# Preparation of a half split in two, with its last eight products behind the buffers' wait, and stores to DRAM on GpSimd's queue

## The chip, the cores and the metric

The kernel runs on one core of a Trainium2 chip. Its engines have an instruction queue each and meet through semaphores: TensorE (PE; PEld is its weight load), VectorE (DVE), ScalarE (ACT), GpSimd (POOL), and SyncE (SP), which in this kernel does nothing but issue DMAs. The metric is device time in microseconds (us), the median of several runs.

## The reference

One layer of a hybrid decoder on T = 1056 tokens (a prompt of 1024, and 8 samples of 4), width 1024, all in float32:

```python
h = rmsnorm(x, norm_mix_g);  z = h @ w_in              # 1024 -> conv, r, k, v, LoRA inputs, gates
ya = silu(layernorm(causal_dwconv(glu(zc)))) @ w_conv_out
xs = zr + (prev - zr) * rw_mu                          # token shift, gives r, k, v, wl, al, gl
kk = normalize(k * rw_k_k);  k = k * (1 + (alr - 1) * rw_k_a)
S_t = S_{t-1} diag(w_t) + (S_{t-1} a_t) b_t^T + v_t k_t^T;  y_t = S_t r_t    # a = -kk, b = kk * alr
yb = ((groupnorm(y) + bonus) * gout) @ w_rw_out
x = x + (gate_a * ya + gate_b * yb) @ w_mix_out
x = x + ConvFFN(rmsnorm(x))                            # 1024 -> 2 x 3072 -> 1024
```

The recurrence on S, with 16 heads of size 64, is done in chunks of 64 tokens.

## The kernel before

Activations lie with channels on partitions and tokens along the free axis, in three blocks of 352 tokens. Each large product is made of three fp32r products (`mm3`: high x high, low x high, high x low), so one output tile of 128 channels is 3 x 3 x 8 = 72 matmuls of 352 columns.

`mixer_a` makes the convolution's inputs, the LoRA parts and the first r, k, v tiles, and stores them to DRAM (`d_cv`, `d_cum`, `d_alr`, `d_gout`, `d_rkv`). `mixer_b` computes the recurrence in 16 halves n (a half is 4 heads x 256 tokens; four halves in a row carry on the state of the same heads). A half goes through these steps:

- `prep(n)` loads k, cum, alr, r, v of the half from DRAM, and makes the decay P by exp (L911, after a memset of P's edges by GpSimd, L910), `kn`, the norms `nin` (L946 and on), the adjusted key `km`, the bonus `bv` (stored to `d_bv`, L977), and the operands E (E0, E1) and BK by products of 64 x 512 (L929, L988 to L990).
- `stage(n)` multiplies E by BK (`w<-E,BK`), takes the result off PSUM to LQ and E (L1012 to L1018; GpSimd clears the edges of LQ, L1015), stores LQ to `dL` (L1026), reads it back spread over 128 lanes as L (L1028), solves a triangular system there by 31 steps of `tm` = L x X (L1034) and X += tm (L1036) on DVE, and stores X to `dX` (L1038).
- `combine(n)` finishes the inverse with small products (D and LQ).
- `chain(n)` runs four chunks one after the other: c and R, UV, S, y. It ends with the eviction `Yev` (L1159).
- `group_norm(n)` normalizes Yev, adds `bvl`, multiplies by `gol`, and stores to `d_y` (L1203).

Around these run further streams: the samples (`samples_in`, `samples_steps`, `samples_state`), the convolution's layer norm (`ln_block`, from `d_cv` to `d_cs`, L399 and L416), the split of y (`s_y`) and the shift state. `drive` walks through the streams with a clock that counts the PE work issued so far. When no stream is due, it issues the next of the fillers: 18 r, k, v tiles (stored at L464), 16 gate tiles (L455), 8 tiles of the convolution's output. The waits between streams are names in a set; `s_prep` holds prep(n) back until chain(n-3) is done, since E and BK have three sets of buffers. L, X and tm have one buffer each. The list that results goes through a scheduler that sets the final order on each engine from dependences and buffers, so the order on one engine is not that of the source.

All DMAs but eight are issued by SP, in order: loads of weights and of the halves, the two passes dL and dX through DRAM that belong to the solve, and all stores. After the last chain come the merge, the mix, the FFN and the output: large products one after the other.

Of the kernel before, what the change touches and what calls it, by code (L numbers as in the profile page):

```python
# [31 lines left out]
class Net:  # L32
# [68 lines left out]
    def build(self):  # L101
        with ExitStack() as es:
# [6 lines left out]
            with ExitStack() as e1:  # L109
# [6 lines left out]
                with ExitStack() as e:  # L116
                    self.t4 = self.pool(e, "t4", 8)
                    self.mixer_a(w0)
# [231 lines left out]
    def conv_taps(self, cv, i):  # L350
# [18 lines left out]
        nc.sync.dma_start(out=self.d_cv[:, i], in_=c[:, :T])  # L369
# [17 lines left out]
    def ln_block(self, b):  # L387
# [28 lines left out]
        nc.sync.dma_start(out=self.d_cs[:, :, s], in_=C)  # L416
# [15 lines left out]
    def conv_out(self, i):  # L432
# [10 lines left out]
        nc.sync.dma_start(out=self.d_ma[i], in_=ga)  # L443
# [12 lines left out]

    def rkv_tile(self, j, n):
# [3 lines left out]
        t = self.T4("krv"[n])  # L461
        c0 = ZR + jj * 128
        yield from self.shifted(self.wjob(self.a["w_in"][0][:, c0:c0 + 128]), jj, t)
        nc.sync.dma_start(out=self.d_rkv[n][j // 2][:, j % 2], in_=t)  # L464
# [16 lines left out]
    def shifted(self, w, j, out, m=128):  # L481
# [6 lines left out]
        def ev(b, s, ps):  # L488
            t0 = b * BW
            nc.scalar.activation(out=out[:m, s], in_=ps, func=AF.Copy, scale=om)  # L490
            n = min(TP - t0, BW)
            add(out[:m, t0 + 1:t0 + n], ps[:, 0:n - 1])
            if b:
                add(out[:m, t0:t0 + 1], bc[:, b - 1:b])
            if n == BW:
                nc.vector.tensor_copy(out=bc[:, b:b + 1], in_=ps[:, n - 1:n])  # L496
            else:
                x = out[:m, TP:T].rearrange("p (b t) -> p b t", t=4)
# [4 lines left out]
                nc.vector.tensor_copy(out=self.shcol[:m, j, 1:9], in_=z[:, :, 3])  # L503
        yield from self.project_g(w, (self.hH, self.hL), 8, ev, m)
# [78 lines left out]
    def lora_out(self, j):  # L583
# [29 lines left out]
        for t, dst in ((cum, self.d_cum), (al, self.d_alr), (go, self.d_gout)):  # L613
            nc.sync.dma_start(out=dst[j // 2][:, j % 2], in_=t)
# [61 lines left out]
    T2N = 12  # L676

    def mixer_b(self):
# [6 lines left out]
        with ExitStack() as e:  # L685
            self.t4 = self.pool(e, "t4b", 2)
# [89 lines left out]
    def s_prep(self):  # L776
        for n in range(self.NH):
            k = [("rkv", j, x) for j in (n // 4 * 2, n // 4 * 2 + 1) for x in range(3)]
            if n > 2:
                k.append(("chain", n - 3))  # L780
# [4 lines left out]
            yield from self.prep(n)  # L785
            self.done.add(("prep", n))
# [47 lines left out]
    def s_shift(self):  # L834
# [3 lines left out]
        for g in range(7):  # L838
# [9 lines left out]
            nc.sync.dma_start(out=self.o["p_shift"][0][:, g * 512:g * 512 + n], in_=st[0:1, :n])  # L848
            nc.sync.dma_start(out=self.o["s_shift"][0][:, g * 512:g * 512 + n], in_=st[1:9, :n])
# [42 lines left out]
    def prep(self, n):  # L892
# [19 lines left out]
        PC = self.sm.tile([128, 8], F32, tag="PC", name="PC", bufs=3)  # L912
# [13 lines left out]
        E = [self.sg.tile([128, 8, 128], F32, tag=f"E{x}", name=f"E{x}") for x in range(2)]  # L926
# [11 lines left out]
        t2 = kn  # L938
        nc.vector.tensor_tensor(out=t2, in0=kn, in1=alr, op=ALU.mult)
# [5 lines left out]
        nin = self.sm.tile([128, 72], F32, tag="nin", name="nin", bufs=3)  # L945
# [21 lines left out]
        for u in range(2):  # L967
# [718 lines left out]
```

## Time and profile before

| | |
|---|---|
| median of 3 runs | 2556.56 us (2546.82 to 2561.31) |
| profiled execution | 2551.31 us, span 2549.6 us |
| mean granted clock of TensorE | 0.911 of full speed |
| busy: PE, DVE, ACT, POOL | 2372.1, 1645.4, 866.1, 91.9 us |
| first solve begins, last chain ends | about 352 us, 1379 us |

The sum of a stage is read from a view that gives each engine's busy time in a stretch; waits are put down to the instruction whose semaphore came last. Between 352 and 1379 us the 16 halves are worked off; before and after that the large products run with no recurrence beside them.

### The profile page before, as it was taken

Reading aid. Unit: us, or ns where it says so; the run is one execution under the profiler, and the core shown is the slowest. Engines: PE = TensorE matmul, PEld = TensorE weight load, DVE = VectorE, ACT = ScalarE, POOL = GpSimd, SP = SyncE. Lnnn points to the kernel's source line nnn. Section 1 sums busy time; section 2 is a strip of 40 time slices with the busy share of each in tenths; the row PEclk is TensorE's granted clock in tenths of the full one; section 3 lists DMA queues with packets and bytes.
Section 4 is the critical chain, followed back from the end, with each engine's and each line's share of the span. In section 5 each row is a group of like instructions: output and inputs, shape, how many; then the busy total and the mean of one; then the engine's idle time right before and its main releaser. Section 6 shows DMA issues by size and latency. Waiting matters only on the chain.

```text
span 2549.6 us, 41402 instructions
## 1 busy us (share of the span) xinstructions
PE 2372.1 (93%) x16094; PEld 2147.3 (84%) x16094; DVE 1645.4 (65%) x4174; ACT 866.1 (34%) x1716; POOL 91.9 (4%) x248
## 2 busy tenths in 40 slices
PE   6789989977798789898999999999999999999998
PEld 5778977766676577677778999999999999999998
DVE  5999766777767876786674344465554555545556
ACT  4234332433344344333344222333221322213225
POOL 2301100000000000000000000000000000000000
PEclk9999987966676788689999999999999999999999
DMA  4124443323232343434344664431111111111111
GB/s 123 48 82 161 157 115 83 89 69 100 77 98 63 81 115 85 104 92 117 85 114 137 215 188 137 127 128 44 44 47 48 43 51 44 47 47 40 54 51 69
DMA packets 307637, 230.61 MB, mean 90 GB/s; under 512 B 90492, under 2 KB 287123, under 8 KB 306921
## 3 DMA queue, kind: packets, MB, share of 16 engines
q1 hardware_dynamic: 307185, 227.80, 30.7%
q8 instruction: 127, 2.08, 0.3%
q14 instruction: 69, 0.57, 0.1%
q0 software_dynamic: 256, 0.17, 0.0%
HBM read 157.45 MB, written 70.45 MB: 89 GB/s over the span
## 4 chain that ended last, share of the span: by engine, by line
PE 58%; DVE 4%; DMA 3%; ACT 1%; issue 0%; SPq 0%; DVEq 0%; ACTq 0%
PE mm L54 50%; PE w L54 3%; DMA L<-dL 2%; PE c L54 1%; PE y L54 1%; PE w L61 1%; DMA hL<-d_y 1%; DVE tm L1034 0%; DVE X L1036 0%; PE w L1427 0%; PE w L1512 0%; DMA dX<-X 0%; DVE E L1018 0%; PE mm L1648 0%; PE w L1533 0%
## 5 line engine op out<-in xcount | busy, mean ns | idle before, releaser
L54 PE MATMUL mm<-hH,whi 128*128 128x352 f32 (+1 forms) x2568 | 878.1, 342 | 10.4 <-DVE bcol L496 9.1
L54 PE MATMUL mm<-hH,wlo 128*128 128x352 f32 (+1 forms) x2568 | 855.7, 335 | 20.6 <-DVE wlo L49 20.6
L54 PE MATMUL mm<-hL,whi 128*128 128x352 f32 (+1 forms) x2568 | 857.0, 334 | 0.2 <-DVE hL L248 0.2
L54 PEld LDWEIGHTS mm<-hH,whi 128*128 128x128 f32 (+1 forms) x2568 | 494.5, 193 | 38.3 <-DVE bcol L496 11.2
L54 PEld LDWEIGHTS mm<-hH,wlo 128*128 128x128 f32 (+1 forms) x2568 | 494.9, 193 | 33.0 <-DVE wlo L49 23.1
L54 PEld LDWEIGHTS mm<-hL,whi 128*128 128x128 f32 (+1 forms) x2568 | 495.9, 193 | 10.0 <-issue 1.2
L48 ACT ACTIVATE whi<-wraw 128x1024 fp32r<-128x1024 f32 (+2 forms) x123 | 126.0, 1025 | 403.5 <-PE mm L54 342.9
L1518 DVE TENSOR_TENSOR u<-mm,rs 128x352 f32<-128x352 f32 x144 | 73.5, 511 | 224.6 <-PE mm L54 224.5
L49 DVE TENSOR_TENSOR wlo<-wraw,whi 128x1024 fp32r<-128x1024 f32 (+2 forms) x123 | 146.2, 1189 | 67.8 <-ACT whi L48 67.7
L359 DVE SCALAR_TENSOR_TENSOR sg<-cu,par,sg 128x1024 f32<-128x1024 f32 x120 | 162.6, 1361 | 1.5
L54 PE MATMUL mm<-fH,whi 128*128 128x352 f32 x504 | 163.4, 324 | 0.0
L54 PE MATMUL mm<-fH,wlo 128*128 128x352 f32 x504 | 162.8, 323 | 0.0
L54 PE MATMUL mm<-fL,whi 128*128 128x352 f32 x504 | 162.7, 323 | 0.0
L1573 DVE TENSOR_TENSOR acc<-mm,acc 128x352 f32<-128x352 f32 x168 | 86.9, 522 | 94.0 <-PE mm L54 94.0
L1034 DVE TENSOR_TENSOR tm<-L,X 128x60 f32<-128x60 f32 (+24 forms) x496 | 101.4, 204 | 44.5 <-DMA L<-dL 39.4
L1548 DVE SCALAR_TENSOR_TENSOR c<-u,par,c 128x1024 f32<-128x1024 f32 x96 | 123.0, 1281 | 8.1 <-ACT c L1544 5.2
L54 PE MATMUL w<-E,BK 64*128 64x128 f32 x512 | 95.9, 348 | 17.8 <-DVE BK L990 11.7
L1109 ACT ACTIVATE SP<-UV,PC 64x64 f32<-64x64 f32 x192 | 64.8, 343 | 119.0 <-DVE UV L1149 104.8
L1036 DVE TENSOR_TENSOR X<-X,tm 128x60 f32<-128x60 f32 (+24 forms) x496 | 101.3, 204 | 5.1
L54 PEld LDWEIGHTS w<-E,BK 64*128 64x128 f32 x512 | 78.9, 239 | 29.9 <-DVE BK L990 12.3
L54 PE MATMUL y<-UV,E 128*64 128x64 f32 x512 | 75.8, 270 | 21.6 <-DVE UV L1149 18.4
L54 PEld LDWEIGHTS mm<-fH,whi 128*128 128x128 f32 x504 | 94.8, 188 | 0.5
(379 smaller groups left out, 3547.7 us busy)
## 6 DMA issues: line engine op xcount, KB each, us to landing
wraw<-w_in SPq DMA_DIRECT2D x50, 512.0 KB
wraw<-w_up SPq DMA_DIRECT2D x48, 512.0 KB
wraw<-w_down SPq DMA_DIRECT2D x32, 384.0 KB
L<-dL SPq DMA_DIRECT2D x16, 512.0 KB
d_alr<-la SPq DMA_DIRECT2D x8, 528.0 KB
d_cum<-lc SPq DMA_DIRECT2D x8, 528.0 KB
d_gout<-lg SPq DMA_DIRECT2D x8, 528.0 KB
d_k<-k SPq DMA_DIRECT2D x8, 528.0 KB
```

The lines of the kernel that those rows point to most:

```text
L48: nc.scalar.activation(out=hi[:, :nk, :m], in_=raw[:, :nk, :m], func=AF.Copy)
L49: (lo_eng or nc.vector).tensor_tensor(out=lo[:, :nk, :m], in0=raw[:, :nk, :m], in1=hi[:, :nk, :m].bitcast(F32), op=ALU.subtract)
L54: self.nc.tensor.matmul(out, l, r, start=start, stop=stop)
L61: self.nc.tensor.transpose(out, x, ident)
L359: nc.vector.scalar_tensor_tensor(out=c[:, 0:TP], in0=u[:, t:t + TP], scalar=self.col("conv_w", t * 4 + i), in1=c[:, 0:TP], op0=ALU.mult, o ...
L1034: nc.vector.tensor_tensor(out=tm[:, :a, :m], in0=L[:, s:s + 1, s + 1:32].to_broadcast([128, a, m]), in1=X[:, :a, s:s + 1].to_broadcast([12 ...
L1036: nc.vector.tensor_tensor(out=X[:, :a, s + 1:32], in0=X[:, :a, s + 1:32], in1=tm[:, :a, :m], op=ALU.add)
L1109: nc.scalar.activation(out=at(SP, u, x), in_=src(x)[:, u], func=AF.Copy, scale=PC[hs[x], 4 * u + c:4 * u + c + 1])
L1518: nc.vector.tensor_tensor(out=u[:, 2 + t0:2 + t0 + m], in0=p, in1=rs[:, t0:t0 + m], op=ALU.mult)
L1548: nc.vector.scalar_tensor_tensor(out=c[:, 0:TP], in0=u[:, t:t + TP], scalar=wt, in1=c[:, 0:TP], op0=ALU.mult, op1=ALU.add)
L1573: nc.vector.tensor_tensor(out=acc[i][:, s], in0=ps[:, :BW], in1=acc[i][:, s], op=ALU.add)
```

## The change

- `prep(n)` is split. What needs no buffer of the stage pool (loads, P, kn, nin, km, bv) no longer waits for chain(n-3). The eight products that write E and BK move into a new function `operands(n)`, issued after that wait. PC and nin get four buffers instead of three, and the T2 buffers are given back at other points.
- `t2` (kn x alr) and `km` are computed in place of alr and k: alr x k once, then a scaled copy and a multiply-add for km and a scaled copy for t2, each per 128 x 256.
- All stores to DRAM but those of the solve (dL, dX), of x2 and of y's output are issued by GpSimd.
- The r, k, v tiles of the fillers and the gate tiles are no longer collected as 128 x 1056 and stored once; each block of 352 tokens has a tile of its own (tag `tb`, three buffers) and a store of its own. The pool t4 has 7 buffers instead of 8, t4b 3 instead of 2, T2 14 instead of 12.
- `tm` is a dense 128 x 80 tile.
- chain(n) waits for the mean and variance steps of group_norm(n-1) before it writes Yev.

```diff
     def gate(self, i, x):
...
-        g = self.T4("gt")
-        yield from self.project_g(w, (self.hH, self.hL), 8,
-                                  lambda b, s, ps: nc.scalar.activation(out=g[:, s], in_=ps, func=AF.Tanh, scale=0.5))
-        nc.sync.dma_start(out=dst, in_=g[:, :T])
+        def ev(b, s, ps):
+            g = self.t4.tile([128, BW], F32, tag="tb", name="gt", bufs=3)
+            nc.scalar.activation(out=g, in_=ps, func=AF.Tanh, scale=0.5)
+            nc.gpsimd.dma_start(out=dst[:, s], in_=g)
+        yield from self.project_g(w, (self.hH, self.hL), 8, ev)
...
         def ev(b, s, ps):
             t0 = b * BW
-            nc.scalar.activation(out=out[:m, s], in_=ps, func=AF.Copy, scale=om)
+            o = self.t4.tile([128, BW], F32, tag="tb", name=out[0], bufs=3) if isinstance(out, tuple) else out[:, s]
+            nc.scalar.activation(out=o[:m], in_=ps, func=AF.Copy, scale=om)
...
+            if isinstance(out, tuple):
+                nc.gpsimd.dma_start(out=out[1][:, s], in_=o)
...
     def s_prep(self):
         for n in range(self.NH):
             k = [("rkv", j, x) for j in (n // 4 * 2, n // 4 * 2 + 1) for x in range(3)]
-            if n > 2:
-                k.append(("chain", n - 3))
...
             yield from self.prep(n)
+            yield from self.wait(*([("chain", n - 3)] if n > 2 else []))
+            self.operands(n)
             self.done.add(("prep", n))
...
-        for x, p in enumerate(hs):
-            nc.vector.tensor_tensor(out=e8(E[x])[p, :, :, 0:64], in0=ch(kn)[p], in1=PP[p, :, :, 0:64], op=ALU.mult)
...
-        t2 = kn
-        nc.vector.tensor_tensor(out=t2, in0=kn, in1=alr, op=ALU.mult)
+
+        nc.vector.tensor_tensor(out=alr, in0=alr, in1=k, op=ALU.mult)
+        t2, km = alr, k
+        for u in range(2):
+            j = 2 * J + u
+            nc.scalar.activation(out=k[:, u], in_=k[:, u], func=AF.Copy, scale=self.oka[:, j:j + 1])
+            nc.vector.scalar_tensor_tensor(out=k[:, u], in0=alr[:, u], scalar=self.col("k_a", j), in1=k[:, u], op0=ALU.mult, op1=ALU.add)
+            nc.scalar.activation(out=alr[:, u], in_=alr[:, u], func=AF.Copy, scale=self.nkk[:, j:j + 1])
...
-            j = 2 * J + u
-            nc.scalar.activation(out=alr[:, u], in_=alr[:, u], func=AF.Identity, scale=self.col("k_a", j), bias=self.oka[:, j:j + 1])
-        nc.vector.tensor_tensor(out=alr, in0=alr, in1=k, op=ALU.mult)
-        km = alr
...
-        nc.sync.dma_start(out=self.d_bv[J][:, :, 256 * q:256 * q + 256], in_=bv[:, :, 0:256])
+        nc.gpsimd.dma_start(out=self.d_bv[J][:, :, 256 * q:256 * q + 256], in_=bv[:, :, 0:256])
...
+    def operands(self, n):
...
+        E = [self.sg.tile([128, 8, 128], F32, tag=f"E{x}", name=f"E{x}") for x in range(2)]
         BK = self.sg.tile([128, 8, 128], F32, tag="BK", name="BK")
         for x, p in enumerate(hs):
+            nc.vector.tensor_tensor(out=e8(E[x])[p, :, :, 0:64], in0=ch(kn)[p], in1=PP[p, :, :, 0:64], op=ALU.mult)
             nc.vector.tensor_tensor(out=e8(E[x])[p, :, :, 64:128], in0=ch(r)[p], in1=PP[p, :, :, 1:65], op=ALU.mult)
             nc.vector.tensor_tensor(out=e8(BK)[p, :, :, 64 * x:64 * x + 64], in0=ch(t2)[p], in1=ch(ip)[p], op=ALU.mult)
             nc.vector.tensor_tensor(out=e8(BK)[p, :, :, 64 - 64 * x:128 - 64 * x], in0=ch(km)[p], in1=ch(ip)[p], op=ALU.mult)
...
         self.carry = Sf
+        yield from self.wait(*([("normed", n - 1)] if n else []))
         self.Y = self.sm.tile([128, 512], F32, tag="Yev", name="Yev", bufs=1)
```

Three places show how the instructions move. The first is DVE between the end of one solve and the start of the next (solves 4 and 5, counted from 0). Before, the products of the next half's stage are taken off PSUM here (w, LQ, E at L1012 to L1018), ahead of the copy that starts X (L1031):

```order
L1012 TENSOR_TENSOR LQ<-w,nin 64x4x64
L1016 TENSOR_TENSOR LQ<-w,tri 64x4x64
L1018 TENSOR_TENSOR E_5624<-w,tri 64x512
L486 SCALAR_TENSOR_TENSOR k<-mm,par_180,k 128x351
L496 COPY bcol<-mm 128x1
L1012 TENSOR_TENSOR LQ<-w,nin 64x4x64
L1016 TENSOR_TENSOR LQ<-w,tri 64x4x64
L1018 TENSOR_TENSOR E_5625<-w,tri 64x512
L1072 STREAM_TRANSPOSE D_5954<-LQ 32x256 x2
L1031 COPY X<-x_2781 128x256
```

After, from the last step of solve 4 (X at L1049) to the start of X for solve 5 (L1043), the same engine has:

```order
L1049 TENSOR_TENSOR X<-X,tm 128x8
L1151 TENSOR_TENSOR UV<-c,nin 64x2x64 x2
L1213 TENSOR_TENSOR y_5505<-y_5505,bvl 128x512
L1162 SCALAR_TENSOR_TENSOR UV<-c,PC,SP 64x64 x4
L1213 TENSOR_TENSOR y_5505<-y_5505,gol 128x512
L1143 COPY R_5877<-c 128x128
L486 SCALAR_TENSOR_TENSOR r<-mm,par_180,r 128x351
L1151 TENSOR_TENSOR UV<-c,nin 64x2x64 x2
L486 SCALAR_TENSOR_TENSOR r<-bcol,par_180,r 128x1
L497 COPY bcol<-mm 128x1
L404 TENSOR_TENSOR lnC<-lnC,w 128x528
L1043 COPY X<-x_2805 128x256
```

The evictions of the next half's LQ stand ahead of this stretch now, among the steps of solve 4. The second place is SP around a load of L. Before, a half's loads (k to v) and stores of a k tile, of y and of the layer norm stand around it:

```order
L1026 DMA dL_4625<-LQ 32x8x32
L900 DMA k<-d_k_480 128x2x256
L900 DMA cum<-d_cum_430 128x2x256
L900 DMA alr<-d_alr_434 128x2x256
L1028 DMA L<-dL_4625 128x1x1024
L900 DMA r<-d_r_484 128x2x256
L900 DMA v<-d_v_488 128x2x256
L464 DMA d_k_481<-k 128x1056
L1203 DMA d_y_425<-y_4710 256x1x256
L399 DMA lnC<-d_cv 128x4x132
L1180 DMA bvl<-d_bv_2840 128x2x256
L416 DMA d_cs<-lnC 512x1x132
```

After, of the stores only those of dL and dX are left on it:

```order
L1040 DMA L<-dL_5272 128x1x1024
L47 DMA wraw<-w_in 128x8x128
L903 DMA k<-d_k_480 128x2x256
L903 DMA cum<-d_cum_430 128x2x256
L903 DMA alr<-d_alr_434 128x2x256
L903 DMA r<-d_r_484 128x2x256
L903 DMA v<-d_v_488 128x2x256
L1038 DMA dL_5716<-LQ 32x8x32 x2
L399 DMA lnC<-d_cv 128x4x132
L1038 DMA dL_5716<-LQ 32x8x32 x2
L1040 DMA L<-dL_5716 128x1x1024
```

SP issues 719 DMAs instead of 953, and GpSimd 322 instead of 8. The third place is GpSimd itself, in the middle of the recurrence. Before, it has memsets (of LQ's edges, of P's edges) and the samples' small products:

```order
L980 COPY sbv<-t_3061 128x64
L910 MEMSET P 128x8
L1015 MEMSET LQ 32x4x32 x8
L910 MEMSET P 128x8
L1015 MEMSET LQ 32x4x32 x4
```

After, stores of r and v blocks, of the bonus (`d_bv`) and of the samples (`d_S`, `d_BT`) stand between them:

```order
L506 DMA d_r_484<-r 128x352 x2
L977 DMA d_bv_2864<-t_3093 256x1x256
L980 COPY sbv<-t_3093 128x64
L1027 MEMSET LQ 32x4x32
L506 DMA d_v_488<-v 128x352
L1027 MEMSET LQ 32x4x32 x3
L1264 DMA d_S_2856<-Sb 128x512
L1284 DMA d_BT_2848<-sB 64x128
L506 DMA d_v_488<-v 128x352
L977 DMA d_bv_2864<-t_3394 256x1x256
L913 MEMSET P 128x8
L1027 MEMSET LQ 32x4x32
```

The memset of P now has stores ahead of it that wait for other engines. Counted over the whole order, DVE has 663 instructions before and 580 after between the end of one solve and the start of the next, in 15 such stretches; stretches of fewer than 40 instructions are 6 before (12, 18, 20, 17, 31, 14) and 12 after (19, 20, 25, 39, 22, 23, 16, 25, 26, 18, 19, 17), and the longest is 89 before and 197 after (between solves 7 and 8). From the first step of solve 0 to the last of solve 15 DVE has 2,614 instructions before and 2,612 after. Of the fillers' products, 152 fewer stand between the first and the last chain after the change; the total on PE is the same.

## Rows read from the trace of the kernel before

**Rows 1.** The page: busy time of each engine, and the PE, DVE and clock lines of the 40 slices of the span.

```profile
PE 2372.1 (93%) x16094; PEld 2147.3 (84%) x16094; DVE 1645.4 (65%) x4174; ACT 866.1 (34%) x1716; POOL 91.9 (4%) x248
...
PE   6789989977798789898999999999999999999998
...
DVE  5999766777767876786674344465554555545556
...
PEclk9999987966676788689999999999999999999999
```

**Rows 2.** Busy time by stage. Columns: stretch, its length, then busy us and number of instructions of PE, PEld, DVE, ACT, POOL, then granted clock, DMA share, GB/s.

```profile
465.00:930.00 465.00, 385.19 (x2990) 313.89 (x2990) 347.10 (x1320) 175.61 (x411) 10.60 (x49) 0.72 0.32 87
930.00:1379.00 449.00, 415.51 (x3439) 334.81 (x3438) 315.55 (x1100) 179.92 (x424) 12.45 (x47) 0.88 0.37 96
465.00:1379.00 914.00, 800.70 (x6427) 648.70 (x6427) 662.65 (x2419) 355.53 (x834) 23.05 (x96) 0.80 0.35 92
...
1690.00:2550.00 860.00, 851.96 (x5290) 835.02 (x5288) 475.29 (x825) 249.87 (x424) 4.47 (x45) 1.00 0.16 49
```

**Rows 3.** The same view for the ten stretches of more than 7 us from the end of a solve (its first store to dX) to the issue of the next load of L: the first and the longest of them, and the sum. (Between the other solves the next load of L is issued within 2 us.)

```profile
508.00:519.00 11.00, 11.00 (x66) 8.47 (x65) 7.35 (x19) 2.95 (x7) 0.71 (x4) 0.50 0.28 42
...
945.00:982.00 37.00, 35.97 (x301) 29.26 (x298) 25.71 (x66) 9.01 (x23) 2.05 (x7) 0.77 0.34 87
...
sum 205.00, PE 188.90 PEld 157.47 DVE 150.60 ACT 55.45 POOL 10.63; mean PE 18.89 PEld 15.75 DVE 15.06 ACT 5.54 POOL 1.06
```

**Rows 4.** The same view, the sum over all 16 stretches from the issue of a load of L to the first store to dX, that is, the solves.

```profile
sum 779.00, PE 670.27 PEld 541.62 DVE 562.65 ACT 311.50 POOL 14.47; mean PE 41.89 PEld 33.85 DVE 35.17 ACT 19.47 POOL 0.90
```

**Rows 5.** The timeline of the longest of those ten stretches: the end of chain 7 on ACT, one of the last products of BK for half 10 on DVE, and SP's issues at the end of solve 9 and at the start of solve 10. Columns: start, duration, what.

```profile
907.78 0.60 ACT L1159 ACTIVATE Yev<-y 128x512 f32<-128x512 f32 x1 [3.79 <-PE y L54]
954.86 0.68 DVE L990 TENSOR_TENSOR BK<-alr,cum 64x512 f32<-64x512 f32 x1
...
944.77 2.59 SPq L1038 DMA_DIRECT2D dX<-X  x4
...
978.20 2.96 SPq L1026 DMA_DIRECT2D dL<-LQ  x4
982.41 0.57 SPq L1028 DMA_DIRECT2D L<-dL  x1
```

**Rows 6.** Waits of DVE, PE and ACT from 465 to 1379 us. Columns: who waits for whom, us in total, times, the longest.

```profile
DVE UV L1138 <- PE c L54: 39.9, 23, 7.5
DVE R L1130 <- PE c L54: 34.7, 26, 5.1
DVE tm L1034 <- DMA L<-dL: 32.5, 8, 10.1
...
PE w L54 <- DVE t L968: 13.3, 4, 6.7
PE mm L54 <- DVE wlo L49: 13.0, 6, 6.1
...
ACT SP L1109 <- DVE UV L1149: 100.1, 46, 9.1
...
ACT P L911 <- POOL P L910: 7.3, 2, 6.5
```

**Rows 7.** Waits of SP's queue from 350 to 1390 us, same columns.

```profile
SPq L1203 <- DVE y L1198: 121.4, 13, 18.1
SPq L1026 <- DVE LQ L1012: 54.2, 14, 16.5
```

**Rows 8.** Groups of instructions: line, engine, operation, count, busy us and mean ns of one; then the chain that ended last, one filler tile of 72 products.

```profile
L963 ACT ACTIVATE alr<-alr,oka,par 128x256 f32<-128x256 f32 (+1 forms) x32 | 17.8, 600 | 9.6 <-DVE kn L939 9.3
L923 ACT ACTIVATE kn<-k,nkk 128x256 f32<-128x256 f32 (+1 forms) x32 | 15.9, 504 | 15.0 <-issue 14.2 <-DVE y L1198 0.4 <-DMA v<-d_v 0.3
L968 DVE SCALAR_TENSOR_TENSOR t<-r,par,alr 128x256 f32<-128x256 f32 (+1 forms) x32 | 15.2, 479 | 0.1
L939 DVE TENSOR_TENSOR kn<-kn,alr 128x512 f32<-128x512 f32 (+1 forms) x16 | 11.2, 701 | 0.1
...
1587.53 11.70 PE mm L54 x72
```

**Rows 9.** The DMAs that GpSimd issues: time on its own queue of one (513 ns), and from issue to landing (5.5 us); then SP's issue of a store of y and of a load.

```profile
L168 POOL DMA_DIRECT2D st<-ffn_dw_w x3 | 1.5, 513 | 0.0
...
st<-ffn_dw_w POOLq DMA_DIRECT2D x3, 24.0 KB, 5.5
...
932.52 0.56 SPq L1203 DMA_DIRECT2D d_y<-y  x1
933.12 0.62 SPq L399 DMA_DIRECT2D lnC<-d_cv  x1
```

More of the change, by code (lines that the diff above doesn't have):

```diff
@@ L116, in build @@
                 with ExitStack() as e:
-                    self.t4 = self.pool(e, "t4", 8)
+                    self.t4 = self.pool(e, "t4", 7)
                     self.mixer_a(w0)
@@ L368, in conv_taps @@
         nc.scalar.activation(out=c[:, TP:T], in_=c[:, TP:T], func=AF.Identity, bias=self.col("conv_b", i))
-        nc.sync.dma_start(out=self.d_cv[:, i], in_=c[:, :T])
+        nc.gpsimd.dma_start(out=self.d_cv[:, i], in_=c[:, :T])
         ps = self.pw_tile()
@@ L415, in ln_block @@
         nc.vector.scalar_tensor_tensor(out=C, in0=Q, scalar=1.0, in1=C, op0=ALU.add, op1=ALU.mult)
-        nc.sync.dma_start(out=self.d_cs[:, :, s], in_=C)
+        nc.gpsimd.dma_start(out=self.d_cs[:, :, s], in_=C)
     def conv_in(self):
@@ L442, in conv_out @@
             out=ga[:, s], in0=ga[:, s], scalar=1.0, in1=ps, op0=ALU.add, op1=ALU.mult))
-        nc.sync.dma_start(out=self.d_ma[i], in_=ga)
+        nc.gpsimd.dma_start(out=self.d_ma[i], in_=ga)
     def gate(self, i, x):
@@ L460, in rkv_tile @@
         jj = (8, 0, 16)[n] + j
-        t = self.T4("krv"[n])
         c0 = ZR + jj * 128
-        yield from self.shifted(self.wjob(self.a["w_in"][0][:, c0:c0 + 128]), jj, t)
-        nc.sync.dma_start(out=self.d_rkv[n][j // 2][:, j % 2], in_=t)
+        dst = self.d_rkv[n][j // 2][:, j % 2]
+        yield from self.shifted(self.wjob(self.a["w_in"][0][:, c0:c0 + 128]), jj, ("krv"[n], dst))
         self.done.add(("rkv", j, n))
@@ L497, in ev @@
             else:
-                x = out[:m, TP:T].rearrange("p (b t) -> p b t", t=4)
+                x = o[:m, n:BW].rearrange("p (b t) -> p b t", t=4)
                 z = ps[:, n:BW].rearrange("p (b t) -> p b t", t=4)
@@ L613, in lora_out @@
         for t, dst in ((cum, self.d_cum), (al, self.d_alr), (go, self.d_gout)):
-            nc.sync.dma_start(out=dst[j // 2][:, j % 2], in_=t)
+            nc.gpsimd.dma_start(out=dst[j // 2][:, j % 2], in_=t)
     def wkv_consts(self):
@@ L685, in mixer_b @@
         with ExitStack() as e:
-            self.t4 = self.pool(e, "t4b", 2)
+            self.t4 = self.pool(e, "t4b", 3)
             self.t2 = self.pool(e, "t2", self.T2N)
@@ L911, in prep @@
         nc.scalar.activation(out=PP[:, :, :, 1:65], in_=ch(cum), func=AF.Exp, scale=-DEC)
-        PC = self.sm.tile([128, 8], F32, tag="PC", name="PC", bufs=3)
+        PC = self.sm.tile([128, 8], F32, tag="PC", name="PC", bufs=4)
         nc.scalar.copy(out=PC.rearrange("p (u c) -> p u c", u=2), in_=PP[:, :, :, 64])
@@ L1029, in stage @@
         X = self.ln.tile([128, 8, 32], F32, tag="X", name="X")
-        tm = self.ln.tile([128, 8, 32], F32, tag="tm", name="tm")
+        tm = self.ln.tile([128, 80], F32, tag="tm", name="tm")
         nc.vector.tensor_copy(out=X, in_=self.x0)
@@ L1173, in group_norm @@
             nc.scalar.activation(out=so, in_=ps[:64, :256], func=AF.Copy)
[L1174 removed]
+            nc.gpsimd.dma_start(out=self.o["p_wkv"][0, 0, 4 * J:4 * J + 4].rearrange("h v k -> v h k"),
                               in_=so.rearrange("p (h k) -> p h k", h=4))
@@ L1184, in group_norm @@
         self.normed(g8(Y), g8(yc), sq=g8(y1.rearrange("p u t -> p (u t)")))
+        self.done.add(("normed", n))
         yield self.W_GN
@@ L1202, in group_norm @@
         else:
-            nc.sync.dma_start(out=self.d_y[J][:, :, s], in_=y1)
+            nc.gpsimd.dma_start(out=self.d_y[J][:, :, s], in_=y1)
     def free(self):
@@ L1248, in samples_in @@
         nc.scalar.activation(out=Sb, in_=ps.rearrange("p (b t) -> p b t", t=64), func=AF.Copy)
-        nc.sync.dma_start(out=self.d_S[j], in_=Sb.rearrange("p b t -> p (b t)"))
+        nc.gpsimd.dma_start(out=self.d_S[j], in_=Sb.rearrange("p b t -> p (b t)"))
         ar = ARs.rearrange("p (o q) t -> p o q t", o=1).to_broadcast([128, 8, 2, 32])
@@ L1268, in samples_in @@
         nc.scalar.activation(out=sB, in_=ps[0:64, 128:256], func=AF.Copy)
-        nc.sync.dma_start(out=self.d_BT[j], in_=sB)
+        nc.gpsimd.dma_start(out=self.d_BT[j], in_=sB)
         yield 2000
@@ L1316, in samples_steps @@
             j = j0 + n
-            nc.sync.dma_start(out=self.d_y[j // 2][:, j % 2, TP:T], in_=y1[:, n])
+            nc.gpsimd.dma_start(out=self.d_y[j // 2][:, j % 2, TP:T], in_=y1[:, n])
     def samples_state(self, j):
@@ L1345, in samples_state @@
             for x in range(2):
-                nc.sync.dma_start(out=self.o["s_wkv"][0, 4 * g:4 * g + 4, 2 * j + x].rearrange("b v k -> v b k"),
+                nc.gpsimd.dma_start(out=self.o["s_wkv"][0, 4 * g:4 * g + 4, 2 * j + x].rearrange("b v k -> v b k"),
                                   in_=so[:, :, 64 * x:64 * x + 64])
```

38 lines of the change are left out of this document (22 added, 16 removed).

## The prediction

> **What bounds the kernel now.** I read the page first. PE is busy for 93% of the span, but the clock line has sixes and sevens in slices 6 to 21 [rows 1]. The view by stages says where: from 465 to 1379 us, while the recurrence runs, PE is busy 800.7 of 914 us at a granted clock of 0.80, with DVE at 662.65 us. From 1690 us on PE is busy 852 of 860 us at 1.00 [rows 2]. So the end of the kernel is bound by PE, and nothing in this change touches its work there. What can move is the recurrence, with 16 solves one after the other through a single set of lanes (L, X, tm), and the fillers beside it.
>
> Then I split that stage by SP's rows. The 16 solves take 779 us, some 49 us each, and DVE is busy 562.65 us of that (72%) [rows 4]. Between them lie ten stretches that sum to 205 us, in which no solve runs [rows 3]. The longest shows why. Chain 7 ends at 907.8 us; prep of half 10 may start only then, and one of its last products, BK, runs at 954.9. The solve before it has stored its X at 944.8, dL leaves at 978.2, and L is asked for at 982.4 [rows 5]. That is 47 us from the chain's end to BK, more than the 37 us that DVE's lanes stand without a solve. In that stretch DVE is busy 25.7 of 37 us, PE 36.0, mostly with fillers [rows 3]: a wait on the chain, bridged with work that could stand elsewhere.
>
> **The change, part by part.** The sum is made against the profiled execution, 2551.3 us, which is 5 below the median of the three runs shown (2556.56).
>
> *Split of prep.* All but eight products are now done before chain(n-3) ends. After it come 8 x 0.68 us (the BK row in [rows 5]) = 5.5 us of DVE, then PE's products and the evictions. The order bears it out: the next half's LQ evictions, which stood behind a solve's last step, stand ahead of it after the change, and stretches under 40 DVE instructions go from 6 to 12. A DVE instruction takes 662.65 / 2419 = 0.274 us [rows 2], so 40 are 11 us. What do the 205 us give back? PE's 188.9 us in them is filler that has to be done somewhere, and at the full clock it is shorter; DVE's 150.6 us is also wanted. What is lost is that DVE stands idle 205 - 150.6 = 54.4 us [rows 3]. Bounds: 0 (the stretches only change places; the order keeps one of 197 instructions between solves 7 and 8) and -205. I take -54, since DVE has the same number of instructions in the recurrence before and after (2,614 and 2,612) and its idle time is what the stretches waste.
>
> *What is late next.* With the gap gone, the load of L stands bare: before, DVE waited for it 8 times, 32.5 us, 4.1 us each [rows 6]; where a gap lay, other work covered it. Six more short gaps make 6 x 4.1 = +25 us (bounds 0, if chain work lies in there as in the order's second piece, and 6 x the longest, 10.1 = 61).
>
> *PE's waits.* In the recurrence PE waits 13.3 us for t (L968, part of the old prep) and 13.0 us for wlo, which DVE makes late [rows 6]. Prep is early now, and blocks stored one by one free their tiles sooner. I take both, -26 us (bounds -26 and 0).
>
> *Clock.* PE at 0.80 over 914 us loses 800.7 x 0.20 = 160 us. The two parts of the stage have 0.72 and 0.88 [rows 2]. If the whole were like the second, 800.7 x 0.08 = 64 us would come back; if like the first, as many would go. I take -25, on the side of less waiting, but nothing here shows what a tighter order is granted, so both ends stay in the range.
>
> *Prep's arithmetic.* Removed for each half: one DVE product of 0.701 us and two ACT steps of 0.600; added: two DVE multiply-adds of 0.479 and four ACT copies of 0.504 [rows 8]. DVE: 16 x (0.958 - 0.701) = +4 us, on the path since DVE works through. ACT: +0.8 us a half; ACT is busy 355.5 of 914 us [rows 2], which hides it. Without that cover it would be 13 us.
>
> *Fillers.* 152 filler products are pushed behind the last chain, where PE is full: a tile of 72 takes 11.70 us [rows 8], so 152 x 0.1625 = 24.7 us there. In the recurrence PE has as much less to do, where DVE waits for PE's chain products (39.9 and 34.7 us, [rows 6]). I take half, +12; bounds 0 and +24.7.
>
> *Stores on GpSimd's queue.* SP loses 234 issues. What it gains is less the issue (0.56 us for a store of y, [rows 9]) than the wait: it stood 121.4 us, 13 times, for group_norm's y [rows 7], and each load or dL behind it stood too. That gain is inside the terms above, because dL's own wait is for its data (54.2 us for LQ). The same waits stand on GpSimd now, and behind them the memset of P's edges and those of LQ. Before, ACT waited only 7.3 us for P [rows 6]. In the changed order that memset has stores of r, v, d_S, d_BT and d_bv ahead of it. With prep early, P is made tens of us before its operands are needed; I charge +8, once more what it was. Bounds: 0, and 16 x 121.4 / 13 = 149. Between ends that far apart I stay near the row that shows the wait itself. An issue by GpSimd takes 0.51 us and lands after 5.5 [rows 9]; 322 of them are 165 us of a queue that is otherwise busy 23 of 914 us, so by its own time it doesn't decide.
>
> The Trainium skill says more here ("SBUF — State Buffer", section "A bandwidth-pool intuition that's wrong (but worth ruling out)"): a DMA whose descriptors GpSimd writes takes about 620 ns alone and about 3100 ns beside a VectorE copy, since GpSimd waits for the port that both use. No trace of before shows such a store under a busy DVE. By that figure, as an estimate, 322 x 3.1 us would be 998 us of GpSimd's queue, more than the recurrence lasts, and the sum would be that of the third rival.
>
> The rest costs nothing on the path: the 80 extra stores move the same bytes, the dense tm changes no count of elements, and chain(n)'s wait for the mean and variance of group_norm(n-1) concerns steps that are a whole chain old.
>
> Sum: -54 + 25 - 26 - 25 + 4 + 12 + 8 = -56, so 2551.3 - 56 = **2495 us**. Its own range, with the gaps' and the clock's terms between nothing and double, is 2425 to 2543.
>
> **Rivals.**
>
> *The recurrence closes up as far as DVE lets it.* With DVE at 95%, its 662.65 us take 697.5; with 12 bare loads of L at 4.1 (49) and prep's 4, the stage lasts 751 instead of 914 us. That is -163, with +25 for the fillers behind and +8 for P: 2421 us. For it: the gaps and DVE's share. Against: inside the solves, where nothing of the change acts, DVE is busy only 72% [rows 4]; its waits for PE's c and ACT's 100.1 us of waiting for UV [rows 6] are the chain's back and forth.
>
> *Nothing moves.* The changed order has the same DVE work in the recurrence, and one stretch of 197 instructions (54 us by 0.274) where the longest had 89. If DVE's order, with chain and prep woven through, is bound by that back and forth, each gap closed comes back as a wait inside a solve. The sum then keeps +4 of arithmetic and a clock as before: 2555 us. The change not doing what it says is part of this.
>
> *GpSimd's queue becomes the chain's brake.* It is in order: P's memset stands behind d_bv and r and v blocks, LQ's memsets behind d_y. If each half's memset is late by what SP waited for y, 121.4 / 13 = 9.3 us [rows 7], that is 149 us over 16 halves, and ACT, which stands before P's exp, has SP's scaling and Yev of the chain behind it (L1109, L1159). If the chain feels two thirds (ACT is idle 61% of the stage, so a third is cover), that is +99 against -64, the sum without its +8 for P: 2551.3 - 64 + 99 = 2586 us. It decides once P's memset is later than the 5.5 us that the products leave, at more than ten halves. For it: the order's third piece, where the store of d_bv stands directly ahead of the memset. Against: prep runs a whole chain early.
>
> A page of the Trainium skill ("DMA: Bandwidth & Descriptors", section "Issuing engines are not separate DMA queues") says that DMAs issued from several engines run on the same 16 DMA engines, and that another issuer saves only its own time to start them. By that, 234 issues of 0.56 us would be at most 131 us of SP's time, and none of the transfers'. SP's wait rows speak for more, since the time lies in waiting at the head of the queue.
>
> **How the numbers follow.** Below 0.5% (13 us) a measurement of this kernel doesn't tell a change from none. Chances: the forecast 0.50, the closed recurrence 0.22, nothing 0.12, GpSimd's brake 0.16. Faster by over 0.5% takes the first two and a little of the third, 0.74; within 0.5% 0.11; slower 0.15. The range reaches to 2400 below the closed recurrence (more clock) and to 2585 at the brake's price. The forecast's own range stands above.
>
> **What would show it.** In the profile of the changed kernel: L's issue within a few us of dX at most halves, and BK's products some 5 us behind a chain's end; tm's waits for L at some 57 us in total instead of 32.5; a clock above 0.80 in the recurrence; the last chain's end near 1300 us instead of 1379, and some 25 us more of fillers behind it; no large wait of ACT for P; SP's queue without waits for y. I am wrong if the solves themselves grow as the gaps close, if the clock falls, or if ACT waits tens of us for P's memset, and GpSimd's issues take several times 0.51 us.

## The result, and the profile after

The changed kernel takes 2536.94 us in the median of 20 runs (2519.59 to 2546.69), the kernel before 2550.75 us in 20 runs beside them. The ratio is 0.9946, with an interval of 0.9927 to 0.9965: 13.8 us faster, where 56 were forecast. The sign was right, the size a quarter.

The page of the changed kernel, same lines as in [rows 1]:

```profile
PE 2341.8 (93%) x16094; PEld 2114.6 (84%) x16094; DVE 1646.8 (65%) x4190; ACT 877.9 (35%) x1748; POOL 263.2 (10%) x562
...
PE   6789998987889689889999999999999999999998
...
DVE  5999777688787877786862344475555545545556
...
PEclk9989997867679789897999999999999999999999
```

This execution (2521.95 us, span 2520.3) was one of the fastest of its kernel. A second profile of it (e1, span 2536.4) lies at the median and is used for the sums below.

The stretches of before: from the start to the first load of L, from there to the last chain's end, and from there to the end of the span. The columns are those of [rows 2].

```profile
0.00:352.00 352.00, 309.04 (x1755) 273.04 (x1755) 291.13 (x438) 136.72 (x236) 62.16 (x93) 0.95 0.36 117
352.00:1379.00 1027.00, 902.17 (x7111) 733.53 (x7110) 732.77 (x2672) 382.49 (x894) 25.10 (x107) 0.80 0.34 91
1379.00:2549.60 1170.60, 1160.86 (x7232) 1140.78 (x7231) 621.54 (x1066) 346.91 (x588) 4.64 (x48) 1.00 0.27 82
```

The same three of the changed kernel, second profile:

```profile
0.00:350.00 350.00, 306.40 (x1736) 270.79 (x1737) 289.33 (x430) 135.94 (x236) 88.46 (x155) 0.95 0.38 119
350.00:1337.00 987.00, 866.18 (x6970) 691.98 (x6969) 734.05 (x2692) 390.57 (x917) 136.45 (x296) 0.82 0.34 92
1337.00:2536.40 1199.40, 1187.60 (x7394) 1167.14 (x7390) 624.18 (x1069) 351.75 (x596) 38.10 (x111) 1.00 0.27 82
```

The recurrence is 40 us shorter (1027 to 987), and what comes behind it is 29 us longer (1170.6 to 1199.4). Read PE's column: behind the chain it gains 26.7 us, the filler products that moved there. In the recurrence its busy time falls by 36.0 us. About 25 of those are the products that left (152 x 0.1625), about 11 the higher clock. PE's idle time there went only from 124.8 to 120.8 us. So of the 40 us, 29 were given back behind the chain.

The gaps did close. In the first profile of the changed kernel L is asked for within 6 us of the solve's end at 13 of 15 places. At eight of them (three before) it is asked for ahead of the store of dX, as here on SP:

```profile
1001.64 0.56 SPq L1040 DMA_DIRECT2D L<-dL  x1
1002.25 2.93 SPq L1051 DMA_DIRECT2D dX<-X  x4
```

Two long stretches are left (columns as in [rows 3]):

```profile
767.00:844.00 77.00, 77.00 (x683) 63.50 (x682) 58.70 (x183) 40.25 (x94) 8.97 (x21) 1.00 0.32 91
1052.00:1082.00 30.00, 27.23 (x226) 23.07 (x227) 19.38 (x51) 10.78 (x25) 6.27 (x17) 0.86 0.49 121
```

They come to 107 us where ten such stretches came to 205 [rows 3]. The first of them is the row to remember. No solve runs for 77 us, DVE idles 18 us, and PE is busy for all 77 us at a clock of 1.00. For PE, this gap is the best stretch of the recurrence.

Waits of the changed kernel in the recurrence (first profile, 450 to 1321 us; columns as in [rows 6]):

```profile
DVE R L1143 <- PE c L54: 40.4, 27, 5.5
DVE UV L1151 <- PE c L54: 27.8, 29, 6.7
DVE tm L1047 <- DMA L<-dL: 13.6, 4, 6.1
...
PE w L54 <- DVE tm L1047: 16.5, 6, 9.4
PE mm L54 <- DVE wlo L49: 11.8, 4, 4.5
...
ACT SP L1122 <- DVE UV L1162: 67.8, 40, 8.5
```

PE's wait for t is gone. Its wait behind the solve's own steps (tm) grew from 9.6 us, which the kernel before has from 465 to 1379 us:

```profile
PE w L54 <- DVE tm L1034: 9.6, 3, 7.1
```

The load of L, which I had expected to stand bare, is waited for less than before.

### The profile page after: what moved, and what is told of

Read it like the earlier page. It is cut to its first block, busy times and chain, and to the rows that moved or that the text cites. A ratio compares the mean times of both kernels' runs of the same rounds, so it can differ in the third digit from the quotient of the medians.

```text
span 2520.3 us, 41895 instructions
## 1 busy us (share of the span) xinstructions
PE 2341.8 (93%) x16094; PEld 2114.6 (84%) x16094; DVE 1646.8 (65%) x4190; ACT 877.9 (35%) x1748; POOL 263.2 (10%) x562
## 4 chain that ended last, share of the span: by engine, by line
PE 78%; DVE 12%; DMA 6%; ACT 2%; issue 2%; SPq 1%; DVEq 0%; ACTq 0%; POOLq 0%
PE mm L54 62%; PE w L54 6%; PE c L54 2%; PE y L54 2%; DMA L<-dL 2%; DVE sg L359 2%; PE w L61 2%; DMA dX<-X 2%; DVE X L1049 1%; DVE tm L1047 1%; DVE wlo L49 1%; DMA d_ma<-ga 0%; SPq L1051 0%; DVE E L1030 0%; DVE UV L1162 0%
## 5 line engine op out<-in xcount | busy, mean ns | idle before, releaser
L1049 DVE TENSOR_TENSOR X<-X,tm 128x60 f32<-128x60 f32 (+24 forms) x496 | 100.4, 202 | 5.3
L54 PEld LDWEIGHTS mm<-fH,wlo 128*128 128x128 f32 x504 | 95.0, 188 | 0.0
```

The lines of the kernel that those rows point to most:

```text
L54: self.nc.tensor.matmul(out, l, r, start=start, stop=stop)
L1049: nc.vector.tensor_tensor(out=X[:, :a, s + 1:32], in0=X[:, :a, s + 1:32], in1=tp, op=ALU.add)
```

## The experiments

Every run is compared with the kernel before on the same chip. "Recurrence" is the stretch from the first load of L to the last chain's end, "behind" the rest; idle is the recurrence less PE's busy time in it. The ratio rests on 6 to 20 runs of each kernel. The other columns are those of one profiled execution each, which can lie off the median of its kernel: the first profile of the changed kernel 15 us below, e14 11 us below, e15 14 us above, the others up to 7 us.

| run | ratio (interval) | recurrence | PE busy, idle in it | clock | behind |
|---|---|---|---|---|---|
| before | 1 | 1027 | 902.2, 124.8 | 0.80 | 1170.6 |
| changed, first profile | 0.9946 (0.9927 to 0.9965) | 972 | 850.0, 122.0 | 0.83 | 1199.3 |
| e1 changed, again | 0.9940 (0.9914 to 0.9966) | 987 | 866.2, 120.8 | 0.82 | 1199.4 |
| e2 stores on SP | 0.9951 (0.9925 to 0.9978) | 985 | 861.5, 123.5 | 0.81 | 1204.9 |
| e3 before, stores on GpSimd | 1.0105 (1.0067 to 1.0144) | 1018 | 890.5, 127.5 | 0.78 | 1196.2 |
| e4 no split | 0.9944 (0.9913 to 0.9975) | 1001 | 887.9, 113.1 | 0.82 | 1171.9 |
| e5 before, room only | 1.0009 (0.9987 to 1.0030) | 1037 | 916.9, 120.1 | 0.80 | 1169.3 |
| e6 12 T2 buffers | 0.9980 (0.9951 to 1.0009) | 979 | 857.9, 121.1 | 0.81 | 1208.1 |
| e7 old km | 0.9884 (0.9853 to 0.9915) | 971 | 852.7, 118.3 | 0.83 | 1199.5 |
| e8 before, dense tm | 1.0014 (0.9988 to 1.0040) | 1023 | 897.0, 126.0 | 0.81 | 1172.5 |
| e9 no split, stores on SP | 1.0042 (1.0021 to 1.0064) | 1044 | 921.5, 122.5 | 0.80 | 1165.5 |
| e10 pause 6600 | 1.0014 (0.9989 to 1.0038) | 1003 | 888.1, 114.9 | 0.81 | 1197.6 |
| e11 old km, pause 6600 | 0.9953 (0.9931 to 0.9974) | 985 | 878.8, 106.2 | 0.81 | 1197.8 |
| e12 before, new km | 1.0046 (1.0020 to 1.0072) | 1017 | 900.0, 117.0 | 0.79 | 1184.3 |
| e13 old km, ACT twice | 0.9961 (0.9927 to 0.9995) | 991 | 871.9, 119.1 | 0.81 | 1201.6 |
| e14 old km, more DVE | 0.9919 (0.9887 to 0.9951) | 972 | 853.1, 118.9 | 0.83 | 1195.6 |
| e15 old km, pause 5400 | 0.9928 (0.9902 to 0.9955) | 990 | 875.7, 114.3 | 0.81 | 1201.9 |
| e16 before, pause 5400 | 1.0112 (1.0070 to 1.0154) | 1057 | 937.0, 120.0 | 0.78 | 1166.4 |
| e17 no split, pause 6600 | 1.0064 (1.0033 to 1.0094) | | | | |
| e18 stores on SP, pause 6600 | 0.9993 (0.9964 to 1.0021) | 997 | 884.0, 113.0 | 0.79 | 1206.8 |

(The profile of e17 is that of its longest execution, 2589.22 us against a median of 2569.61, so its stretches are left out.)

**e1, the changed kernel again.** 

> The changed kernel once more, for a second profile. Theory L (a ledger of TensorE: outside the recurrence its time is fixed, inside it the end comes when work at the granted clock plus idle time is through): the last chain ends near 1321 us again, the stretch behind it lasts near 1199 us again, and what differs from the first profile (2521.95 us) differs by the granted clock of the recurrence alone; 2537 us. Rival R (the first profile was of another kind of run): the last chain ends 10 us or more later while the clock is the same.

Measured: 2532.61 us; the last chain ends at 1337 us, the rest takes 1199.4. The end of the chain moved by 16 us between two executions of one program, with the clock of the recurrence at 0.83 and 0.82 and the same idle time (122.0, 120.8). Behind the chain the two agree. The forecast end at 1321 us was missed. What theory L says of the difference holds, as far as two profiles show: it is PE's busy time at another clock, 850.0 and 866.2 us for the same products.

**e2, all stores on SP.**

```diff
-            nc.gpsimd.dma_start(out=self.d_y[J][:, :, s], in_=y1)
+            nc.sync.dma_start(out=self.d_y[J][:, :, s], in_=y1)
...
```

> The changed kernel with all 19 store statements back on SP's queue. Theory P (the gain is the split's): 2537 us, within 5. Theory Q (the gain is the stores', SP no longer waits for y): back to 2550 us, SP waiting about 120 us for y again. Theory L adds: only if TensorE's idle time or its time at the lower clock in the recurrence falls does the time fall; 61 more filler products stand behind the last chain than in the changed kernel, which is no loss by itself.

Measured: 2535.94 us, the same as with GpSimd. Beside the split, the queue of the stores is worth nothing. Theory Q's simple form falls. SP's wait for y did not come back in full, though: it is 38.2 us here, where it was 121.4 before [rows 7].

**e3, the kernel before with stores on GpSimd.** The same edit the other way round.

> The kernel before with its stores issued by GpSimd and nothing else changed. Theory P: 2551 us, within 5. Theory Q: about 2537 us. If GpSimd's queue costs the chain something (the third rival), 2560 us or more, with ACT waiting tens of us for the memset of P.

Measured: 2570.82 us, 1% slower. ACT's wait for P's memset is not among its large ones. What did change: 140 products more stand behind the chain (24 us there), and the clock of the recurrence fell to 0.78, so the recurrence got only 9 us shorter.

**e4, prep waits as a whole.**

```diff
+            if n > 2:
+                k.append(("chain", n - 3))
...
             yield from self.prep(n)
-            yield from self.wait(*([("chain", n - 3)] if n > 2 else []))
             self.operands(n)
```

> The changed kernel with the wait for chain(n-3) ahead of all of prep again, everything else as changed. Theory P: 2551 us or a little more, the last chain's end back near 1375 us, stretches without a solve as long as before, and fewer fillers behind the chain. Theory Q: 2537 us.

Measured: 2530.74 us. Its recurrence and the rest:

```profile
350.00:1351.00 1001.00, 887.92 (x7138) 718.61 (x7136) 734.94 (x2695) 394.00 (x927) 140.50 (x303) 0.82 0.35 93
1351.00:2522.90 1171.90, 1160.73 (x7222) 1140.36 (x7221) 621.30 (x1066) 346.80 (x587) 34.28 (x104) 1.00 0.27 82
```

The gaps are back in part: the stretches of more than 7 us without a solve sum to 160 us (the longest 33, 32, 28 and 22), against 107 in the changed kernel and 205 before. The chain ends 14 us later than in e1, the fillers are back in the recurrence, and the time is that of the changed kernel. Theory P falls in this order: with 107 or with 160 us of gaps, the end is the same.

**e5, e6, e8, room.** The kernel before with narrow blocks, dense tm and 14 T2 buffers (e5); the changed kernel with 12 (e6); the kernel before with the dense tm (e8). The edit of e6:

```diff
-    T2N = 14
+    T2N = 12
```

> The kernel before, with only the changes of room: tiles of 352 columns for r, k, v and gates (stored block by block, by SP as before), the dense tm, and 14 T2 buffers instead of 12. No split, no stores on GpSimd, old arithmetic. Theory B (the two more T2 buffers carry the gain; prep, group_norm and the samples wait less for room): about 2535 us, the last chain's end near 1350 us. Rival K (the new arithmetic of km and t2): 2550 us.

> The changed kernel with 12 T2 buffers as before. Theory B: back to about 2550 us. If the split gives something of its own when room is short: 2540 us. If the buffers are worth nothing: 2535 us. 40 more filler products stand behind the last chain than in the changed kernel, worth 6.5 us by the ledger if nothing else falls.

> The kernel before with the dense tm alone. If tm's layout carries the gain: 2537 us, with tm and X shorter than 204 ns. Theory B and rival K: 2550 us.

Measured: 2554.65, 2546.11 and 2554.03 us. Room alone gives nothing (e5, e8), so theory B falls as I put it. Taking two buffers from the changed kernel costs it some 0.3 to 0.4%, with intervals that just overlap. That the rest uses the room is possible and not shown: e10 below moves the time by more with no change of room.

**e7, the old arithmetic of km and t2.**

```diff
-        nc.vector.tensor_tensor(out=alr, in0=alr, in1=k, op=ALU.mult)
-        t2, km = alr, k
...
+        t2 = self.T2([128, 2, W], "t2n")
+        nc.vector.tensor_tensor(out=t2, in0=kn, in1=alr, op=ALU.mult)
+        for u in range(2):
+            j = 2 * J + u
+            nc.scalar.activation(out=alr[:, u], in_=alr[:, u], func=AF.Identity, scale=self.col("k_a", j), bias=self.oka[:, j:j + 1])
+        nc.vector.tensor_tensor(out=alr, in0=alr, in1=k, op=ALU.mult)
+        km = alr
```

> The changed kernel with the arithmetic of km and t2 as before (t2 in a T2 buffer of its own). Rival K: 2550 us. Theory B: 2535 us, or 4 us less by the count of DVE's work that I put at +4.

Measured: 2521.06 us, 0.9884, the fastest kernel of the study and faster than both. The new arithmetic costs the change about as much as the change gains. Three of its groups in the changed kernel (columns as in [rows 8]):

```profile
L945 ACT ACTIVATE alr<-alr,nkk 128x256 f32<-128x256 f32 (+1 forms) x32 | 15.7, 511 | 12.5 <-DVE k L944 12.2
L944 DVE SCALAR_TENSOR_TENSOR k<-alr,par,k 128x256 f32<-128x256 f32 (+1 forms) x32 | 15.2, 485 | 0.9 <-ACT k L943 0.8
L943 ACT ACTIVATE k<-k,oka 128x256 f32<-128x256 f32 (+1 forms) x32 | 14.9, 502 | 4.6 <-DVE alr L939 4.6
```

ACT does 30.6 us in these where it did 17.8 in L963 [rows 8], and stands 17 us in front of them for DVE, where it stood 9 in front of L963. How much of that the chain feels, these rows don't say.

**e9, both named parts undone.** The edits of e2 and e4 together.

> The changed kernel with both of its named parts undone: prep waits for chain(n-3) as a whole, and all stores are on SP. What is left: the eight operand products at prep's end, the new arithmetic, narrow blocks, dense tm, 14 T2 buffers, four PC and nin, Yev's wait. Either part alone changed nothing in the changed kernel (0.9944 without the split, 0.9951 without GpSimd's stores, against 0.994 with both). If each of them can do the other's work (either SP free or prep early frees the loads): 2550 us with both undone. If neither counts and the rest carries the gain: 2532 us.

Measured: 2560.76 us, 1.0042. With both gone the gain is gone; with either one there, it is there. Either could do the other's work, or the orders differ by accident. The next runs ask that.

**e10, e11, e12, the order shifted, and the arithmetic.**

```diff
-    W_NIN, W_BV, W_GN, W_STAGE = 6000, 8000, 12000, 0
+    W_NIN, W_BV, W_GN, W_STAGE = 6600, 8000, 12000, 0
```

> The changed kernel with one planning number changed: the pause before the norms of prep 6600 instead of 6000. No instruction more or less, the same 7186 filler products behind the last chain; only the order shifts a little. Theory O (the order's accidents decide how often TensorE falls to the lower clock, and parts are worth what their order happens to be): the time differs from 2533 us by 8 us or more, in either direction. Rival A (what a part costs is its own work): within 4 us of 2533.

> The changed kernel with the old arithmetic of km and t2 and the same pause of 6600; its 7186 filler products behind the last chain are as many as in the kernel of the run before. Rival A: 12 to 14 us less than that run, as the old arithmetic brought with the pause of 6000. Theory O: the distance is another, less than 6 us or of the other sign.

> The kernel before with the new arithmetic alone. Rival A: 2551 + 13 = 2564 us. Theory O: no rule; by the ledger the 72 products more behind the last chain add 12 us there, and the recurrence shortens by as much or not.

Measured: 2550.21, 2536.31 and 2559.94 us. Both theories hold in part. The pause alone costs the changed kernel 0.7%, all that it had gained, without an instruction more. The old arithmetic, though, is 0.6% faster in the shifted order too, and the new one costs the kernel before 0.5%. By the ratios, three orders give 14, 16 and 12 us. In the third, e12, 74 products more stand behind the chain, which is 14 us longer, while the recurrence is 10 us shorter; so its 12 us need not be the arithmetic's own.

**e13, e14, which engine pays for the arithmetic.**

```diff
             nc.scalar.activation(out=kn[:, u], in_=k[:, u], func=AF.Copy, scale=self.nkk[:, 2 * J + u:2 * J + u + 1])
+            nc.scalar.activation(out=kn[:, u], in_=k[:, u], func=AF.Copy, scale=self.nkk[:, 2 * J + u:2 * J + u + 1])
```

> The changed kernel with the old arithmetic, in which each half makes its two scaled copies of kn twice: ACT does 2 x 0.504 us more per half, a little more than the new arithmetic adds there, and nothing else is added. If the new arithmetic's price (12 to 15 us in three comparisons) is ACT's work in front of the chain's steps: 0.9884 + 0.005 = 0.993 to 0.995 of before. If it is DVE's work or the hand-overs between ACT and DVE: 0.988 to 0.990.

> The changed kernel with the old arithmetic, in which each half does one of its multiply-adds of t1 twice: DVE does 0.479 us more per half, nearly double what the new arithmetic adds there (0.257). If the price is DVE's work: 0.9884 + 0.010 = 0.998 of before. If ACT's work or the hand-overs: 0.988 to 0.991 (8 us of DVE work, partly hidden).

Measured: 2543.76 us (0.9961) and 2525.99 us (0.9919). The recurrence of e7, then that of e13, which has two ACT copies a half more, then that of e14:

```profile
347.00:1318.00 971.00, 852.67 (x6968) 684.71 (x6967) 730.21 (x2680) 380.43 (x890) 135.03 (x296) 0.83 0.34 93
```

```profile
350.00:1341.00 991.00, 871.91 (x6954) 697.52 (x6952) 729.69 (x2678) 390.68 (x914) 133.51 (x295) 0.81 0.34 91
```

```profile
346.00:1318.00 972.00, 853.06 (x6982) 682.83 (x6980) 736.80 (x2696) 381.40 (x890) 137.65 (x296) 0.83 0.35 94
```

10 us of ACT work more, and the recurrence of e13 is 20 us longer, at nearly the same idle time and a lower clock. The ratio rises by 0.0077, more than the 0.005 to 0.007 that I gave ACT; DVE's work, at nearly twice the amount, brings 0.35%, between my two cases, and its interval overlaps that of e7. This points to ACT. It isn't settled, since a shift of the order can be as large.

**e15, e16, the size of such accidents.** The pause at 5400, with the old arithmetic and in the kernel before.

> The changed kernel with the old arithmetic and the pause before the norms of prep at 5400 instead of 6000. A candidate for the fastest. If a longer pause costs steadily (6600 cost 0.7% with either arithmetic): 0.982 of before. If 6600 was an accident of the order: anything from 0.984 to 0.998.

> The kernel before with the pause at 5400 and nothing else; 37 filler products fewer stand behind the last chain. If the order's accidents are worth some 10 us whatever the kernel: a ratio off 1 by 0.004 or more, in either direction. If a neutral change of the order is worth nothing in the kernel before: 0.998 to 1.002.

Measured: 2529.51 us (0.9928) and 2578.72 us (1.0112). A longer and a shorter pause both measure worse than 6000 (at 5400 the intervals just overlap), so this is no steady effect. In the kernel before, a pause of 600 less costs 28 us, as much as GpSimd's stores seemed to cost it in e3; so that 1% may be the order's too. Its recurrence:

```profile
354.00:1411.00 1057.00, 936.95 (x7147) 762.10 (x7146) 732.73 (x2675) 381.75 (x896) 24.69 (x107) 0.78 0.33 89
```

With 36 products more than before (some 6 us), PE is busy 35 us longer, at a lower clock and with 5 us less idle time.

**e17, e18, each named part once more, in another order.** The edits of e4 and e2 with the pause of 6600; to be set against e10 (1.0014).

> The changed kernel without the split (prep waits for chain(n-3) as a whole) and with the pause of 6600, to set against e10 (pause 6600 with the split, 1.0014). If the split is worth nothing of its own whatever the order: 0.998 to 1.005. If e4's 0.9944 was an accident that hid the split's gain: 1.007 or more.

> The changed kernel with all stores on SP and the pause of 6600, against e10 (1.0014). If the queue of the stores is worth nothing of its own beside the split: 0.998 to 1.005. If it is worth something: 1.007 or more; if GpSimd's stores cost the changed kernel something: under 0.997.

Measured: 2569.61 us (1.0064) and 2547.83 us (0.9993). The stores' queue is worth nothing here as well. Taking the split out costs 0.5% in this order, between my two bounds, with intervals that just overlap. So the split is worth 0 in one order and perhaps 13 us in the other.

## Why the prediction was wrong

**The step that failed: "its idle time is what the stretches waste".** I put the gaps' -54 us on DVE's idle time, as if DVE set the end of the recurrence. The gaps closed from 205 to 107 us. But with 160 us of them open again the time is the same (e4), and in the other order that costs 0.5% (e17 against e10). So closing them is worth something between nothing and 13 us.

DVE's idle time isn't what counts: in the recurrence it goes from 235 us (e14) to 324 (e16). PE's idle time lies between 106 and 128 us in every profile, with gaps or without, and behind the last chain the time is PE's work and 10 to 13 us. A gap that PE fills with fillers at full clock (77 us at 1.00 above) takes nothing from PE's account, which holds its idle time and its time at the lower clock. Against the kernel before, the whole change took 4 us of idle time and some 11 by the clock; against e4, closing the gaps took none of the idle time (120.8 and 113.1 us). I had the row for it: 188.9 of 205 us busy in the gaps [rows 3].

This account is not a proof that PE alone sets the end. That busy and idle time add up to the length is true of every engine, and only the steadiness of PE's idle time is a finding. The chain that ended last (from the last instruction back, at each step, to what released it) lies, in the recurrence of e1, on PE for 608 of 987 us, on DVE for 201 and on DMA transfers for 120. And ACT's work seems to lengthen the recurrence in e13, which shows in PE's account only as a lower clock. What in an order lowers the clock, no run shows.

**Fillers, +12.** The whole is paid: 26.7 us behind the chain. "Half back" has no place in PE's account, where the recurrence gets shorter by the same work.

**Arithmetic, +4.** Mis-sized: 12 to 16 us in three comparisons. I took DVE's 4 as the price and hid ACT's 13 us behind its idle share. ACT's work seems to be what costs (e13); that it costs in front of the chain's short steps is not shown.

**PE's waits, -26.** The wait for t went, that for wlo stayed (11.8 us), and others grew, that for tm from 9.6 to 16.5: PE's idle time fell by 4 in all.

**Clock, -25.** The direction was right, 0.80 to 0.82 or 0.83. It is 11 us in e1 and 27 in the first profile, so that execution alone would have made this term look right.

**Bare loads of L, +25.** Wrong: DVE's wait fell from 32.5 to 13.6 us. L is asked for ahead of the store of dX more often now, at eight places instead of three. That this is the reason is not shown: in e4 it is so at four, and the wait is 9.6 us.

**P's memset, +8.** Nothing: ACT's wait for it is 7.1 us in all against 7.3. GpSimd's stores took up to 734 ns each on its queue (means by group), beside a DVE that was busy 76% of the time from 450 to 1321 us:

```profile
L506 POOL DMA_DIRECT2D d_r<-r x24 | 13.3, 553 | 88.3 <-DVE bcol L497 34.3 <-issue 22.5 <-DVE shcol L504 18.6
L1218 POOL DMA_DIRECT2D d_y<-y x16 | 10.9, 682 | 76.8 <-issue 39.5 <-DVE nin L952 15.3 <-ACT k L943 7.9
L416 POOL DMA_DIRECT2D d_cs<-lnC x8 | 5.9, 734 | 28.1 <-DVE tm L1047 12.1 <-DVE lnC L415 7.2 <-DVE X L1049 3.1
...
d_k<-k POOLq DMA_DIRECT2D x24, 176.0 KB, 2.9
```

The 3100 ns of the Trainium skill's page "SBUF — State Buffer" (section "A bandwidth-pool intuition that's wrong (but worth ruling out)") do not show on the queue. The page states them beside a VectorE copy, and copies are 31 of DVE's 660 busy us here, so these stores hardly test it, and my estimate of 998 us had charged it to all of them. The time from issue to landing, 1.6 to 4.6 us by group, doesn't decide it either: no run has these stores with DVE at rest. The other rule, that of "DMA: Bandwidth & Descriptors" in the section "Issuing engines are not separate DMA queues", agrees with e2 and e18: another issuer saved nothing that the time shows. The same edit between e4 and e9 goes with 1%, and why is open.

**The range.** The sum's range was to run with the gaps' and the clock's terms between nothing and double. With both at nothing the sum is 2574 us, with both doubled 2416, so 2425 to 2543 doesn't follow from it, and that the measured time lies inside is luck.

In sums of e1: before the recurrence -2, in it -40, behind it +29: -13. **The rivals:** the closed recurrence and GpSimd's brake didn't come. "Nothing moves" was the nearest in size: the closed gaps did come back in part inside the solves, whose stretches sum to 807 us in the first profile after (931 us from the first L to the last dX, less 107 of long gaps and 17 of short ones) against 779 [rows 4].

What stays open: why neither part counts alone while both undone cost 1% (e9). An accident of the order, of the size of e10 and e16, would do, and I have no run that excludes it. The same holds for the 13.8 us of the whole change: a pause moved by 10% takes all of it back, so no part of the change is shown to have earned it.

## What to carry to other kernels

Where one engine has fillers for every wait of the others, keep the account of that engine first: its work outside, and inside its busy time at the granted clock plus its idle time. A wait elsewhere is worth only what it takes from these, and work pushed behind the last chain is paid in full. Before a part of a change is credited with half a percent, shift the order by a planning number that means nothing: here that moved the time by 0.7 and 1.1%. On an engine that a serial chain passes through, don't count added small steps as free because the engine is only 40% busy: here they seemed to cost full price or more.

## What the runs showed that I had not expected

One program differs by 27 us between runs, and the granted clock goes with it: among the 20 runs of the changed kernel the shortest, 2519.59 us, has the mean clock 0.930, and the longest, 2546.69 us, has 0.916. In the recurrence a lower clock need not go with more idle time: e16 has less idle time than the kernel before (120.0 and 124.8 us) and a lower clock (0.78 and 0.80).
